# Attention's products with values at the end of a step and one step later, with out-projection chunks moved one step and q's projection over five steps

## The chip, the cores and the metric

The kernel runs on one core of one Trainium2 chip, as one launch. The metric is the device time of that launch in microseconds. The median of three runs before the change is 913.32 us (913.21 to 914.18). One further execution was profiled; its own time was 913.42 us.

## What is computed

Two layers on an input of 256 tokens by 1024 features, all in float32. Each layer is a half-weighted SwiGLU block, a mixer, and a second SwiGLU block, with a layer norm after each of the three. The mixer of layer 0 is a bidirectional chunkwise mLSTM, that of layer 1 a windowed attention. The change lies in the attention alone:

```python
def window_attention(x, w_in, sink, w_out):          # 16 query heads, 4 key/value heads of 64
    p = x @ w_in                                      # q | k | v
    ...
    s = jnp.einsum('bnqkgd,bnskd->bnkgqs', q, kw) * (HEAD_DIM ** -0.5)
    s = s - slopes[:, :, None, None] * dist           # ALiBi
    s = jnp.where(valid, s, MASK_VALUE)               # |t - s| <= 128
    m = jnp.maximum(jnp.max(s, axis=-1, keepdims=True), sink_l)
    pe = jnp.exp(s - m)
    attn = pe / (jnp.sum(pe, axis=-1, keepdims=True) + jnp.exp(sink_l - m))
    o = jnp.einsum('bnkgqs,bnskd->bnqkgd', attn, vw).reshape(B, S, nq)
    return o @ w_out
```

## The kernel before

Float32 accuracy is had from pairs: a float32 operand is split into a rounded high part (a copy on ScalarE) and a low part (a subtraction on VectorE), and a product is three matmuls, high by high, high by low and low by high (`mm3`). Names ending in `_hi` and `_lo` are such pairs. Weights come by DMA into `w_raw` or `s_raw` tiles; `W.high` makes `w_hi` on ScalarE, `W.low` makes `w_lo` on VectorE, and `W.done(.., PU[st], True)` in the attention loop makes up to `PU[st]` high parts, whose low parts follow in `W.lows()`. All engines run their instructions in the order in which the program issues them, so the order of the Python code is the order of each queue. Most vector, scalar and tensor calls go through a recording helper and carry its line, L180; tiles are told apart by their names.

The attention (`attn`) treats the 16 heads as eight pairs j. The first part projects k, v and the first four pairs of q. Then a hand-written software pipeline of eleven steps st runs (L1552 to L1586). A pair goes through four stages, one step apart:

- `scores(j)` in step j: twelve short matmuls of 64 rows into two PSUM banks (`pw<-kT,q`), then on VectorE four fused bias, mask and minimum operations per pair (`sc`, `nm`), then on ScalarE four exponentials with row sums (`sc<-sc,nm`), and `es`.
- `scale(j)` in step j+1: the reciprocal of the sum, and on GpSimd four multiplications of 128 by 256 (`sc<-sc,sm`, L1489). Except for pair 0, the sum and the reciprocal are on GpSimd too (L1485, L1486).
- `turn(j, sb, p)` in step j+2, for sb 0 and 1: four transposes on TensorE (`pw<-ident,sc`), a copy on ScalarE (`pr` high) and a subtraction on VectorE (`pr` low). In steps 2 to 7 the first turn stands ahead of the scores of the step and the second one in the midst of `scores`, after its matmuls (`between`).
- `values(j)` in step j+3, as the first thing of that step: twelve matmuls with v (`pw<-pr,v`), whose result is copied into the place of q's pair j in `qT` (`q_hi<-pw` on ScalarE, `q_lo<-pw` on VectorE).

These stages take their PSUM tiles from `wbank`, four banks in one rotation (`pw`); q's projection and the accumulators of the out-projection take theirs from `ybank` (`py`). A bank is taken again once its last reader is done.

What is left of TensorE's time in a step is filled by `work`, a list of small parts from `fill`. For steps 0 to 3 these are parts of `q_rest`, which projects q's pairs 4 to 7: part i is one `mm3` with 256 columns (three matmuls `py<-xT,w`), 32 parts in all, and every eighth part ends in a copy and a subtraction into `qT`. Parts 0 to 5 run ahead of the loop, and `QC` (L33) says where each step begins: parts 6 to 11 in step 0, 12 to 19 in step 1, 20 to 27 in step 2 and 28 to 31 in step 3. In steps 4 to 10 the parts are those of `out_proj` for chunk c = st - 4: one part is an `mm3` with 512 columns for one half of the tokens and one half of the outputs (`py<-w,q`), four parts for chunks 0 and 1 (`CT`) and two for the others. Of the parts of a step, the first `FB[st]` stand ahead of the transposes (L36), the rest at the end.

After the loop, `tail` adds what is left of the out-projection and does the layer norm. The second feed-forward block of the layer follows.

Of the kernel before, what the change touches and what calls it, by code (L numbers as in the profile page):

```python
# [9 lines left out]
F32 = mybir.dt.float32  # L10
# [19 lines left out]
FIRST = 12  # L30
RING = 10
PU = [2, 0, 1, 2, 1, 2, 1, 1, 0, 1, 2, 4]
QC = [2, 12, 20, 28, 32]  # L33
QX = 6
SW = 1
FB = [1, 0, 1, 0, 2, 0, 0, 0, 1, 1, 2]  # L36
CT = [0, 1]
EX = [1, 2, 2, 2, 2, 2, 2, 2]
RS = [0, 0, 1, 0, 1, 0, 0, 0, 0, 0, 0, 3, 0, 0, 1, 0, 1, 0, 1, 0, 0, 0, 2, 0, 0, 0, 1, 0, 1, 2, 0, 0, 0, 1, 0, 0, 2, 0, 1, 1, 0, 0, 0, 0, 2, 2, 0, 1]
# [405 lines left out]
def trunk_kernel(ctx: ExitStack, tc: tile.TileContext, x, ffn_w_in, ffn_w_out, ln_g, ln_b, ml_w_in, ml_gate_b,  # L445
                 ml_norm_g, ml_w_out, at_w_in, at_sink, at_w_out, out):
    nc = Paced(tc.nc)
# [174 lines left out]
    def pair(p, *idx):  # L622
        return p[0][idx], p[1][idx]

    def wbank(shape=(128, 512)):
        return psum.tile(list(shape), F32, name="pw", tag="pw", bufs=4)
# [4 lines left out]
    A = slice(None)  # L631
# [32 lines left out]
    def load_ln(room, l, n):  # L664
        t = []
        for name, w in (("g", ln_g), ("b", ln_b)):
            a = room("ln_" + name)
            src = w[l, n]
            nc.load(a, bass.AP(tensor=src.tensor, offset=src.offset, ap=[[0, 128], [1, D]]))
            t.append(a)  # L670
        return t
# [663 lines left out]
    def attn(l, n, pending, last):  # L1335
        with ExitStack() as ph:
# [3 lines left out]
            def both(shape, name, bufs=1):  # L1340
                return tuple(tile_(shape, FR, name + e, bufs=bufs) for e in ("_hi", "_lo"))
# [30 lines left out]
            qT = both([128, 8, S], "q")  # L1372
# [28 lines left out]
            def k_turn(t):  # L1401
                p = ybank((128, 4, 128))
                for g in range(4):
                    nc.tensor.transpose(p[:, g], kd[t][:, g].rearrange("p a d -> p (a d)"), ident)
                split_evac(pair(kT, A, A, tok(t)), p)

            def q_turn(t):
                p = ybank((128, 4, 128))
                for j in range(4):
                    nc.tensor.transpose(p[:, j], qd[t][:, j], ident)  # L1410
                split_evac(pair(qT, A, slice(0, 4), tok(t)), p)
# [3 lines left out]
            def q_rest(part):  # L1415
                for i in part:
                    g, f, k = i // 16, i // 8 % 2, i % 8
                    if k == 0:
                        qpart[g] = (W.take(2) if f == 0 else qpart[g][0], ybank((128, S)))
                    pcs, p = qpart[g]  # L1420
                    mm3(p, pair(pcs[k // 4], A, k % 4, tok(f)), pair(xT, A, k), k == 0, k == 7)
                    if k == 7:
                        split_evac(pair(qT, A, 4 + 2 * g + f), p, qs_col[:, 2 * g + f:2 * g + f + 1])
                        if f == 1:
                            del qpart[g]
# [5 lines left out]
            def flush(n):  # L1431

                for d, src in lows[:n]:
                    nc.vector.tensor_sub(d[1], src, d[0].bitcast(F32))
                del lows[:n]
# [43 lines left out]
            def scale(j):  # L1479
                sm, es = stat.pop(j)  # L1480
                if j == 0:
                    nc.vector.tensor_add(sm, sm, es)
                    nc.vector.reciprocal(sm, sm)
                else:
                    nc.gpsimd.tensor_add(sm, sm, es)  # L1485
                    nc.gpsimd.tensor_tensor(sm, sm, minus_one, op=OP.pow)  # L1486
                for t in range(2):
                    for a in range(2):
                        nc.gpsimd.tensor_scalar(sc[j, t][:, a], sc[j, t][:, a], sm[:, t, a:a + 1], 1.0,  # L1489
                                                op0=OP.mult, op1=OP.mult)  # L1490

            def turn(j, sb, p):
                for t in range(2):
                    for a in range(2):
                        nc.tensor.transpose(p[:, a, tok(t)], sc[j, t][:, a, tok(sb)], ident)
                r = W.room(f"pr{sb}", TAGS[2 + sb]).bitcast(FR).rearrange("p (e a s) -> p e a s", e=2, a=2)
                d = (r[:, 0], r[:, 1])
                nc.scalar.copy(d[0], p)
                lows.append((d, p))
                pr[j, sb] = d  # L1500

            lows, sums = [], {}

            def values(j):
                p = wbank((128, S))
                terms = [(sb, a, e, f) for sb in range(2) for e, f in ((0, 0), (1, 0), (0, 1)) for a in range(2)]
                for n_, (sb, a, e, f) in enumerate(terms):
                    v = va[sb][:, j // 2].rearrange("p s d -> p (s d)")
                    at = 128 * e + 64 * (1 - a)
                    nc.tensor.matmul(p, v[:, at:at + 128], pr[j, sb][f][:, a], start=n_ == 0, stop=n_ == len(terms) - 1)  # L1510
                sums[j] = p
                for sb in range(2):
                    del pr[j, sb]
                    W.back(TAGS[2 + sb], 1)

            y = []

# [2 lines left out]
            def out_part(c, t, o):  # L1520
                if not y:
                    y.extend([ybank() for _ in range(2)] for _ in range(2))
                if c not in wo:
                    wo[c], = W.take_rows(1)
                mm3(y[t][o], pair(qT, A, c, tok(t)), pair(wo[c][1], A, 0, slice(o * 512, o * 512 + 512)), c == 0, False)
# [6 lines left out]
            def parts(f_, *args):  # L1532

                if f_ is q_rest:
                    return [lambda i=i: q_rest([i]) for i in args[0]]
                return [lambda t=t, o=o: out_part(args[0], t, o) for t in args[1] for o in range(2)]
# [8 lines left out]
            k_turn(1)  # L1545
            q_rest(range(QC[0]))
            q_turn(1)
            q_rest(range(QC[0], QX))
            fill = {n_: (q_rest, range(max(QX, QC[n_]), QC[n_ + 1])) for n_ in range(4)}
            for c in range(7):  # L1550
                fill[c + 4] = (out_proj, c, (0, 1) if c in CT else (0,))
            for st in range(11):  # L1552
                if st == 2:
                    gb = load_ln(lambda name: tile_([128, D], F32, name), l, n)
                if 0 <= st - 3 < 8:
                    values(st - 3)
                    o = sums.pop(st - 3)
                    d = pair(qT, A, st - 3)
                    nc.scalar.copy(d[0], o)
                    nc.vector.tensor_sub(d[1], o, d[0].bitcast(F32))  # L1560
                if 0 <= st - 1 < 8:
                    rest()
                    scale(st - 1)
                if st == 8:
                    kT.clear()
                    W.back(TAGS[4], 2)
                late = None
                work = parts(*fill[st]) if st in fill else []
                if 0 <= st - 2 < 8:
                    for f_ in work[:FB[st]]:  # L1570
                        f_()
                    work = work[FB[st]:]
                    p0, p1 = wbank((128, 2, S)), wbank((128, 2, S))
                    turn(st - 2, 0, p0)
                    late = lambda: turn(st - 2, 1, p1)
                    if st >= 8 or not SW:
                        late()
                        late = None
                held = [wo[c][0] for c in wo if c not in CT]
                W.done(min([W.used - (2 if qpart else 0)] + held), PU[st], True)  # L1580
                if st < 8:
                    rest = scores(st, late)
                flush(2)
                W.lows()
                for f_ in work:
                    f_()  # L1586
            nc.scalar.preload_act_table(AF.Silu)
            W.done(0, PU[11])
            wo[7], = W.take_rows(1)
# [7 lines left out]
    for j, (kind, l, i, n) in enumerate(stages):  # L1597
        last = j == len(stages) - 1
        bound[0] = j
        nc.filler = W.fill if kind == "ffn" else None  # L1600
        if kind == "ffn":
            pending = ffn(l, i, n, pending, last)
        elif kind == "mlstm":
            pending = mlstm(l, n, pending, last)
        else:
            pending = attn(l, n, pending, last)
# [29 lines left out]
```

## Time and profile before

| what | value |
|---|---|
| median of the runs | 913.32 us |
| time of the profiled execution | 913.42 us |
| its span, first to last instruction | 911.7 us |
| TensorE matmuls, busy | 902.5 us (99%), 4459 of them |
| VectorE, ScalarE, GpSimd, busy | 804.4, 573.1, 152.5 us |
| matmuls of `values` (`pw<-pr,v`) | 96, first 681.1 us, last 717.6 us |
| exponentials of `scores` | 32, first 671.2 us, last 710.1 us |
| scaling on GpSimd (L1489) | 32, first 675.0 us, last 714.2 us |

Times inside the profile count from the start of the span. The eleven steps lie between 669 and 719 us. A matmul's duration is longer than the distance to the next one, since matmuls overlap in the array; how fast TensorE goes is read from the starts. A row of the view in order of time stands for a run of like instructions that follow each other (xN), with the time from the first one's start to the last one's end; brackets give idle time before it and what ended it. The rows "PEld" are TensorE's weight loads.

### The profile page before, as it was taken

How to read it: one execution, taken by the hardware profiler on the slowest of the kernel's cores; microseconds unless marked ns; L12 is line 12 of the kernel's file. 1: busy time of each engine (PE TensorE's matmuls, PEld its weight loads, DVE VectorE, ACT ScalarE, POOL GpSimd, SP SyncE). 2: the span in 40 equal slices, each digit the busy share in tenths (PEclk: the TensorE clock that was granted, in tenths of full speed). 3: DMA queues.
4: the chain of work that ended last, by engine and by line, in shares of the span. 5: the costliest groups of instructions: out<-in, count | busy, mean ns of one | idle time of the engine just before them, and what ended most of it. 6: DMA issues, size and time to landing. Idle time of an engine off the chain costs nothing.

```text
span 911.7 us, 12563 instructions
## 1 busy us (share of the span) xinstructions
PE 902.5 (99%) x4459; PEld 757.4 (83%) x4459; DVE 804.4 (88%) x971; ACT 573.1 (63%) x793; POOL 152.5 (17%) x192
## 2 busy tenths in 40 slices
PE   9999999999999999999999999999999999999996
PEld 7888888889988888888888888888898888888885
DVE  5999999886799898999888899998869889899886
ACT  5776777356664656776646676764569566676660
POOL 0111123113211011212011111110425301111110
PEclk9999999999999999999999999999999999999999
DMA  8999998546637898997868989986534587899851
GB/s 281 367 328 259 288 274 215 162 137 186 208 111 246 296 234 244 290 285 234 241 193 269 259 257 283 272 223 197 159 119 140 163 293 221 204 298 278 252 138 47
DMA packets 100703, 208.53 MB, mean 229 GB/s; under 512 B 6904, under 2 KB 21264, under 8 KB 100640
## 3 DMA queue, kind: packets, MB, share of 16 engines
q1 hardware_dynamic: 82368, 173.04, 54.2%
q0 software_dynamic: 17696, 33.65, 22.3%
q10 hardware_dynamic: 576, 1.05, 0.3%
q8 instruction: 35, 0.57, 0.3%
q14 instruction: 28, 0.23, 0.1%
HBM read 206.65 MB, written 1.05 MB: 228 GB/s over the span
## 4 chain that ended last, share of the span: by engine, by line
PE 98%; DVE 1%; DMA 0%; issue 0%; DVEq 0%
PE pw L180 64%; PE py L180 35%; DMA x<-in_x_dram 0%; DVE x L180 0%; DVE stats L180 0%; DVEq L1632 0%; DVE mv L180 0%; DVE rs L180 0%
## 5 line engine op out<-in xcount | busy, mean ns | idle before, releaser
L180 DVE TENSOR_TENSOR w_lo<-w_raw,w_hi 128x1024 fp32r<-128x1024 f32 (+1 forms) x213 | 255.2, 1219 | 26.6 <-ACT w_hi L180 24.8
L180 ACT CAST w_hi<-w_raw 128x1024 fp32r<-128x1024 f32 (+1 forms) x213 | 218.9, 1049 | 80.3 <-PE py L180 21.7
L180 DVE TENSOR_TENSOR w_lo<-s_raw,w_hi 128x1024 fp32r<-128x1024 f32 x192 | 228.6, 1219 | 18.3 <-ACT w_hi L180 18.2
L180 ACT CAST w_hi<-s_raw 128x1024 fp32r<-128x1024 f32 x192 | 196.6, 1054 | 58.4 <-PE py L180 23.3
L180 PE MATMUL pw<-w_hi,xT_hi 128*128 128x512 f32 x480 | 189.5, 396 | 0.0
L180 PE MATMUL pw<-w_hi,xT_lo 128*128 128x512 f32 x480 | 187.0, 391 | 0.0
L180 PE MATMUL pw<-w_lo,xT_hi 128*128 128x512 f32 x480 | 186.7, 390 | 0.0
L122 POOL DMA_DIRECT2D s_raw<-in_ffn_w_in_dram x64 | 77.4, 1211 | 484.1 <-DVE s_raw L180 226.3
L180 PE MATMUL py<-w_hi,h_hi 128*128 128x512 f32 x349 | 138.2, 396 | 0.0
L180 PE MATMUL py<-w_hi,h_lo 128*128 128x512 f32 x349 | 136.2, 390 | 0.0
L180 PE MATMUL py<-w_lo,h_hi 128*128 128x512 f32 x349 | 136.0, 390 | 0.0
L180 PEld LDWEIGHTS pw<-w_hi,xT_lo 128*128 128x128 f32 x480 | 90.0, 188 | 19.1
L180 PEld LDWEIGHTS pw<-w_lo,xT_hi 128*128 128x128 f32 x480 | 90.3, 188 | 18.6 <-DVE w_lo L180 1.2
L180 PEld LDWEIGHTS pw<-w_hi,xT_hi 128*128 128x128 f32 x480 | 90.1, 188 | 17.4 <-ACT w_hi L180 0.2
L180 PE MATMUL pw<-w_hi,S_hi 128*128 128x512 f32 x256 | 99.7, 390 | 0.0
L180 PE MATMUL pw<-w_lo,S_hi 128*128 128x512 f32 x256 | 99.7, 389 | 0.0
L180 PE MATMUL pw<-w_hi,S_lo 128*128 128x512 f32 x256 | 99.7, 389 | 0.0
L180 PEld LDWEIGHTS py<-w_hi,h_lo 128*128 128x128 f32 x349 | 65.5, 188 | 14.1
L180 DVE TENSOR_TENSOR s_raw<-s_raw,s_raw 128x1024 f32<-128x1024 f32 x64 | 76.8, 1219 | 0.3
L180 PEld LDWEIGHTS py<-w_lo,h_hi 128*128 128x128 f32 x349 | 65.7, 188 | 13.0
L180 PEld LDWEIGHTS py<-w_hi,h_hi 128*128 128x128 f32 x349 | 65.6, 188 | 12.7
L180 PEld LDWEIGHTS pw<-w_hi,S_lo 128*128 128x128 f32 x256 | 48.1, 188 | 10.0
(205 smaller groups left out, 1122.7 us busy)
## 6 DMA issues: line engine op xcount, KB each, us to landing
s_raw<-in_ffn_w_in_dram SPq DMA_DIRECT2D x96, 512.0 KB, 8.0
w_raw<-in_ffn_w_out_dram SPq DMA_DIRECT2D x88, 512.0 KB, 6.1
w_raw<-in_ffn_w_in_dram SPq DMA_DIRECT2D x64, 512.0 KB, 5.7
s_raw<-in_ffn_w_in_dram POOLq DMA_DIRECT2D x64, 512.0 KB, 8.3
w_raw<-in_ml_w_in_dram SPq DMA_DIRECT2D x24, 512.0 KB, 4.6
w_raw<-in_ffn_w_in_dram SPq DMA_DIRECT2D x32, 256.0 KB, 6.0
w_raw<-in_at_w_in_dram SPq DMA_DIRECT2D x12, 512.0 KB, 4.8
w_raw<-in_ml_w_out_dram SPq DMA_DIRECT2D x8, 512.0 KB, 4.1
```

The costliest lines, as they stand in the source:

```text
L122: self.nc.gpsimd.dma_start(ap, source, accum_op=OP.add)
L180: r = f(out, *args, **kw)
```

## The change

`values(j)` copies its result itself. In steps 3 to 7 it is called as the last thing of the step, after the parts of `work`, where it was called as the first thing; its pair is still st - 3. In steps 8 to 10 it stays at the start, behind `VB[st - 8]` parts of `work` (one in step 8, none in 9 and 10). On TensorE's queue `values(0)` so stands between the parts of step 3 and the first transposes of step 4, where it stood ahead of the transposes of step 3; the same holds for pairs 1 to 4.

The chunks of the out-projection go to the steps in `OC`: chunk 0 in step 5, 1 in 6, 2 in 7, 3 and 4 in 8, 5 in 9 and 6 in 10. Parts 6 to 31 of q's projection are spread over five steps: 6 to 11, 12 to 17, 18 to 23, 24 to 27 and 28 to 31. `FB[4]` is 0, where it was 2. Counts of instructions stay the same on every engine.

```diff
-QC = [2, 12, 20, 28, 32]
+QC = [2, 12, 18, 24, 28, 32]
+OC = [5, 6, 7, 8, 8, 9, 10]
+VB = [1, 0, 0]
...
-FB = [1, 0, 1, 0, 2, 0, 0, 0, 1, 1, 2]
+FB = [1, 0, 1, 0, 0, 0, 0, 0, 1, 1, 2]
...
             def values(j):
...
-                sums[j] = p
                 for sb in range(2):
                     del pr[j, sb]
                     W.back(TAGS[2 + sb], 1)
+                d = pair(qT, A, j)
+                nc.scalar.copy(d[0], p)
+                nc.vector.tensor_sub(d[1], p, d[0].bitcast(F32))
...
-            fill = {n_: (q_rest, range(max(QX, QC[n_]), QC[n_ + 1])) for n_ in range(4)}
+            fill = {n_: parts(q_rest, range(max(QX, QC[n_]), QC[n_ + 1])) for n_ in range(5)}
             for c in range(7):
-                fill[c + 4] = (out_proj, c, (0, 1) if c in CT else (0,))
+                fill.setdefault(OC[c], []).extend(parts(out_proj, c, (0, 1) if c in CT else (0,)))
             for st in range(11):
...
-                if 0 <= st - 3 < 8:
+                work = fill.get(st, [])
+                if st >= 8:
+                    for f_ in work[:VB[st - 8]]:
+                        f_()
+                    work = work[VB[st - 8]:]
                     values(st - 3)
-                    o = sums.pop(st - 3)
-                    d = pair(qT, A, st - 3)
-                    nc.scalar.copy(d[0], o)
-                    nc.vector.tensor_sub(d[1], o, d[0].bitcast(F32))
...
-                work = parts(*fill[st]) if st in fill else []
...
                 W.lows()
                 for f_ in work:
                     f_()
+                if 3 <= st < 8:
+                    values(st - 3)
```

On the queue of SP, which issues the loads, one 512 KB load and one pair of 256 KB loads of the next block's `w_raw` come ahead of `s_raw` loads that they followed before: the tiles of `pr` lie in the rooms of `s_raw`, and are given back where `values` is called. The queue of GpSimd is the same. On ScalarE and VectorE only the places of the copies into `qT` change.

2 lines of the change are left out of this document (1 added, 1 removed).

## The prediction

> **What bounds the kernel.** I read the head of the page first, then the chain of work that ended last, then the busy time by stretches.
>
> ```profile
> span 911.7 us, 12563 instructions
> PE 902.5 (99%) x4459; PEld 757.4 (83%) x4459; DVE 804.4 (88%) x971; ACT 573.1 (63%) x793; POOL 152.5 (17%) x192
> ...
> PE 98%; DVE 1%; DMA 0%; issue 0%; DVEq 0%
> ```
>
> ```profile
> 680.00:700.00 20.00, 20.00 (x154) 17.62 (x153) 18.51 (x47) 19.06 (x56) 11.19 (x23) 1.00 0.40 133
> ```
>
> TensorE is busy 99% of the span, 98% of the final chain is TensorE, and it has no idle time to give away. The second fence is 680 to 700 us, in the midst of the attention's steps (window, length, then busy us and instructions of PE, PEld, DVE, ACT, POOL, the granted clock, DMA share, GB/s): TensorE 20.00 of 20 us, but ScalarE 19.06 and VectorE 18.51. So here three engines are nearly full at once. The change takes no matmul away and adds none; it can only remove or add waits of TensorE, and a wait comes out at the end one for one. Busy time cannot show these waits, since a matmul's record is longer than the step to the next; I take them from distances between starts in the order of time.
>
> **What can be won** is small: the waits inside `values`, twelve matmuls that begin while a low part of `pr` is still being made.
>
> ```profile
> 687.40 0.30 PEld L180 LDWEIGHTS pw<-pr,v 128*128 128x128 f32 x2 [0.19 <-DVE pr L180]
> ```
>
> ```profile
> 681.10 1.60 PE L180 MATMUL pw<-pr,v 128*128 128x256 f32 x12
> 682.54 0.60 PE L180 MATMUL pw<-ident,sc 128*128 128x128 f32 x4
> ...
> 685.96 1.94 PE L180 MATMUL pw<-pr,v 128*128 128x256 f32 x12
> 687.74 0.40 PE L180 MATMUL py<-w_hi,q_hi 128*128 128x512 f32 x1
> ...
> 692.45 1.80 PE L180 MATMUL pw<-pr,v 128*128 128x256 f32 x12
> ...
> 703.50 1.80 PE L180 MATMUL pw<-pr,v 128*128 128x256 f32 x12
> ...
> 708.47 1.80 PE L180 MATMUL pw<-pr,v 128*128 128x256 f32 x12
> ```
>
> The first call (pair 0) runs without a wait: 1.60 us, and 682.54 - 681.10 = 1.44 us from its start to the next work. Against 1.60, pair 1 loses 0.34 us, and pairs 2, 4 and 5 0.20 us each. One step later their `pr` is long done, so at most 0.94 us can come back. That is 0.1% of the run.
>
> **What it costs, first place: step 2.** The transposes of step 2 need pair 0 scaled by GpSimd.
>
> ```profile
> 675.02 1.85 POOL L1489 TENSOR_SCALAR sc<-sc,sm 128x256 f32<-128x256 f32 x4 [16.34 <-DVE sm L180]
> ```
>
> ```profile
> 676.55 0.71 PE L180 MATMUL pw<-ident,sc 128*128 128x128 f32 x4
> 677.18 0.39 PE L180 MATMUL pw<-kT_hi,q_hi 64*128 64x256 f32 x2
> ```
>
> ```profile
> 674.08 0.48 DVE L180 SCALAR_TENSOR_TENSOR q_lo<-py,qs_col,q_hi 128x256 fp32r<-128x256 f32 x1
> ```
>
> The four scalings end at 676.87, one every 0.46 us; the four transposes start at 676.55 and take 0.71, against 0.60 at 682.54. So today TensorE arrives just as the last scaling ends: two queues in step, no slack. With `QC` cut from eight parts to six in step 1, TensorE has two parts less ahead of these transposes. A part costs 0.36 us (twelve matmuls, four parts, from 684.45 to 685.96 in the rows further down, less 0.08 for the first). GpSimd does not come earlier: it waits for VectorE's `sm`, which follows the `q_lo` at 674.08 and the work ahead of it, and nothing on any engine is changed up to there. TensorE comes 0.72 us earlier and waits 0.72.
>
> **Second place: step 3.** Its first transposes wait for pair 1 in the same way.
>
> ```profile
> 678.87 0.20 POOL L1485 TENSOR_TENSOR sm<-sm,es 128x4 f32<-128x4 f32 x1 [2.00 <-ACT es L180]
> ...
> 680.29 1.84 POOL L1489 TENSOR_SCALAR sc<-sc,sm 128x256 f32<-128x256 f32 x4
> ```
>
> Today TensorE reaches them at 682.54, after the scalings (680.29 + 1.84 = 682.13). In the new order the two further parts that left step 2 (0.72) and `values(0)` (1.44) are no longer ahead of them, and TensorE is there 2.16 us earlier, at 680.38. GpSimd's start hangs on ScalarE's `es`, behind exponentials of pair 1 that nothing moves. The fourth transpose can start at 682.19, a semaphore's 0.06 us after 682.13; today it starts at about 682.87 (the scores follow at 683.07, 0.2 later). With 0.1 us to refill the array after a wait, the scores of step 3 start at 682.45, 0.62 before today's 683.07. But four parts (1.44) and `values(0)` (1.44) have not been done by then. Loss so far: 2.88 - 0.62 = 2.26 us, 0.72 of it from step 2.
>
> **Third place: the bank of `values(0)` in step 4.** The second transposes of a step take the bank that the last `values` filled, and wait until VectorE's `q_lo<-pw` has read it. This wait exists today, by a hair:
>
> ```profile
> 684.03 0.42 PEld L180 LDWEIGHTS pw<-ident,sc 128*128 128x128 f32 x4 [0.19 <-DVE q_lo L180]
> ```
>
> ```profile
> 683.04 0.35 ACT L180 CAST q_hi<-pw 128x256 fp32r<-128x256 f32 x1
> 683.29 0.48 ACT L180 ACTIVATE es<-nm,sink 128x2 f32<-128x2 f32 x2
> 683.67 0.57 ACT L180 CAST pr<-pw 128x512 fp32r<-128x512 f32 x1
> 684.14 2.00 ACT L180 CAST w_hi<-w_raw 128x1024 fp32r<-128x1024 f32 x2
> 686.03 0.58 ACT L180 CAST pr<-pw 128x512 fp32r<-128x512 f32 x1
> 686.51 0.52 ACT L180 ACTIVATE sc<-sc,nm 128x256 f32<-128x256 f32 x1
> ...
> 688.50 0.47 ACT L180 ACTIVATE q_hi<-py,qs_col 128x256 fp32r<-128x256 f32 x1
> ```
>
> ```profile
> 686.65 0.69 DVE L180 TENSOR_TENSOR pr<-pw,pr 128x512 fp32r<-128x512 f32 x1 [0.15 <-ACT pr L180]
> 687.26 2.35 DVE L180 TENSOR_TENSOR w_lo<-w_raw,w_hi 128x1024 fp32r<-128x1024 f32 x2
> 689.53 0.48 DVE L180 SCALAR_TENSOR_TENSOR q_lo<-py,qs_col,q_hi 128x256 fp32r<-128x256 f32 x1
> 689.92 0.41 DVE L180 TENSOR_TENSOR q_lo<-pw,q_hi 128x256 fp32r<-128x256 f32 x1
> ```
>
> Today the copy of pair 0 stands early: after the exponentials of step 2, ahead of everything of step 3. Its place is now that of the last row, behind all of step 3. On ScalarE, with the `q_hi<-pw` gone from 683.04 (0.25 us), the first `pr` copy starts at 683.42, two `w_hi` end at 685.89, the second `pr` at 686.36. On VectorE then: `pr` low until 687.00, two `w_lo` 2.27 us more (687.26 to 689.53), `q_lo<-pw` 0.41: done at 689.69. (On ScalarE four exponentials, 1.99 us, and `q_hi` end at 688.6, in time.) The transposes can start at 689.75.
>
> ```profile
> 683.07 0.39 PE L180 MATMUL pw<-kT_hi,q_hi 64*128 64x256 f32 x2
> ...
> 684.04 0.66 PE L180 MATMUL pw<-ident,sc 128*128 128x128 f32 x4
> 684.45 0.36 PE L180 MATMUL py<-xT_hi,w_hi 128*128 128x256 f32 x1
> ...
> 689.12 0.60 PE L180 MATMUL pw<-ident,sc 128*128 128x128 f32 x4
> ...
> 690.57 0.66 PE L180 MATMUL pw<-ident,sc 128*128 128x128 f32 x4
> ```
>
> TensorE's arrival, from 682.45: scores 0.91 (683.07 to 684.04 less today's wait of 0.06), transposes 0.41, four parts 1.51, `values(0)` 1.44, first transposes of step 4 0.53, scores 0.91: 688.16. It waits 1.59 us, with the scores of pair 4 already done and everything else queued behind it: its own copy of `pr`, the four parts of step 4, `values(1)`.
>
> Balance there: 689.75 against 690.57 today, 0.82 earlier, with four parts (1.43), `values(1)` (1.44) and two out-projection parts (687.74 to 689.12, 1.38) still to do. 4.25 - 0.82 = 3.43 us behind. Today's waits up to that point, pair 1's 0.34 among them, are already in this.
>
> **After that.** Of today's later waits, pairs 2, 4 and 5 give back 0.60. In steps 5 and 6 the same bank is level.
>
> ```profile
> L180 DVE CUSTOM_DVE_ANT_0 sc<-pw,dist,neg_sink 128x256 f32<-128x256 f32 x32 | 14.0, 479 | 2.7 <-PE pw L180 2.1 <-POOL sm L1485 0.6
> ```
>
> From one `q_lo<-pw` to the next, with one `w_lo` between them, VectorE needs four `sc` of 14.0/32 = 0.44, two `pr` of 0.61, the `w_lo` of 1.13 and two `q_lo` of 0.4: 4.9 us; TensorE, from second transposes to second transposes with the four parts of step 4, needs 0.41 + 1.51 + 1.44 + 0.53 + 0.91 = 4.8. In the next round VectorE has two `w_lo`, 6.0, and TensorE the four out-projection parts of step 5 (2.75) instead of 1.51: 6.0. I take 0.1 for both together, between 0 and 0.5. In step 7 TensorE has the same 6.0 us, and VectorE one `w_lo` less. From `values(6)` on TensorE's order is the old one, so the loss is carried to the end.
>
> The loads that now come later are the `s_raw` ones, a step at most, some 5 us.
>
> ```profile
> L180 ACT CAST w_hi<-s_raw x14: 1049/1052/1061, 748.9 to 787.8; 128x1024 fp32r<-128x1024 f32 x14
> ...
> L118 SPq DMA_DIRECT2D s_raw<-in_ffn_w_in_dram x12: 367/463/840, 711.3 to 779.9; - x12
> ```
>
> Issued from 711.3, first read at 748.9: nothing. Without that cover, 5 us. The copies into `qT` are as many as before.
>
> **Sum:** 3.43 - 0.60 + 0.1 = +2.9 us. From the profiled 913.42 that is 916.3; the median, 913.32, lies 0.1 lower, which changes nothing. Two parts could still be wrong by their bounds: the two early waits (2.26) by 0.4, if a transpose follows its scaling by more or less than 0.06; the third by 0.5, the length of half a `w_lo`. Own range: 915.4 to 917.2.
>
> **Rivals.**
>
> *The bank wait comes back in steps 5 and 6.* For it: VectorE's and TensorE's sums are within 0.1 us there, and VectorE's include no wait of its own. Against: in step 4 it starts late by a whole step, in the later ones only by what is left. If it falls behind by half a `w_lo` (0.6) in both, +1.1: 917.4. Chance 0.11.
>
> *The third wait does not come about.* If the transposes of step 4 got a bank other than that of `values(0)`, 1.59 us fall away: 914.7, within 0.2%. For it: four banks rotate. Against: the row at 684.03, where today's order, too, waits for `q_lo`. Chance 0.09.
>
> *Not slower: GpSimd and ScalarE move forward along with TensorE.* The place is the scaling of pairs 0 and 1. If its start came 0.7 us earlier in step 2, and 1.5 earlier in step 3, nothing would be lost, the bank would be free too, and 0.94 us is won: 912.5. It decides from the point where `sm` starts before 674.5. Against: everything ahead of it keeps its place. Chance 0.04.
>
> *The clock drops.* At the start of the span TensorE runs at half pace:
>
> ```profile
> 1.71 3.25 PE L180 MATMUL py<-ident 128*128 128x128 f32 x14 [1.71 <-DVE ident L180]
> ...
> 5.87 1.04 PE L180 MATMUL py<-ident 128*128 128x128 f32 x8
> ```
>
> Fourteen transposes take 3.25 us there, eight take 1.04 a little later. Should the waits of steps 2 to 4, with transposes between them, bring such a stretch back once, 3.5 us at half pace cost 1.7: 918.0. Against: the longest wait is 1.6 us, and the granted clock is 1.00 in this stretch. Chance 0.05. The Trainium skill, "TensorE: Matmul & The Clock Gate", part 1, speaks against this change in just this way: it puts the fall to half clock after an idle window of about 3.4 us. By that rule waits of 1.6 us with matmuls between them are too short, so it would agree with 916.3 and not with 918.0; its remark that transposes do not count as full activity leaves some doubt.
>
> **Chances.** Forecast 0.68, bank in steps 5 and 6 0.11, clock 0.05, no third wait 0.09, not slower 0.04; 0.03 for what I have not seen, 0.02 of it faster. A change under 0.2% (1.8 us) can't be told from none by a measurement of this kernel. Slower: 0.68 + 0.11 + 0.05 = 0.84; same: 0.09 + 0.04 + 0.01 = 0.14; faster 0.02. The range takes in both neighbours: 914.6 to 917.9.
>
> **What would show it.** In the new profile: the four transposes of step 2 about 0.45 us apart, at GpSimd's pace, beginning near 676; the same in step 3, ending near 682.2; and in step 4 a gap of 1.4 to 1.7 us ahead of the second transposes, ended by VectorE's `q_lo`. No `pw<-pr,v` of pairs 1 to 5 should wait for `pr`. I am wrong if GpSimd's scalings move by more than 0.2 us in steps 2 and 3, or if waits appear outside steps 2 to 6.

## The result and the profile after

The changed kernel takes 916.29 us (median; 915.76 to 918.92), beside it the kernel before 913.86 us (913.21 to 914.79): 1.0036 times as long, 95% interval 1.0023 to 1.0049. It is slower, and the forecast of 916.3 us holds. That the median meets it to 0.01 us is luck: beside it the kernel before took 913.86 us and not the 913.32 that the forecast went by, so the difference is 2.43 us, where 2.9 was forecast. The profiled execution took 917.62 us, though, more than the median and more than the forecast, and its profile shows where. First the head of the page and the shares of the final chain.

```profile
span 915.9 us, 12561 instructions
PE 904.6 (99%) x4459; PEld 759.6 (83%) x4459; DVE 804.5 (88%) x971; ACT 574.2 (63%) x793; POOL 152.9 (17%) x192
...
PE 95%; DVE 3%; issue 1%; POOL 0%; ACT 0%; DVEq 0%; POOLq 0%
```

The work is the same and TensorE again "99% busy"; only the chain tells that something is lost, with TensorE at 95% of it instead of 98%. Now the rows that the forecast named, the transposes of steps 2, 3 and 4, and those of step 5, in the order of time on TensorE (in the changed kernel the recording helper's line is L182, and the scaling's L1491):

```profile
675.42 1.42 PE L182 MATMUL pw<-ident,sc 128*128 128x128 f32 x4
...
680.40 1.23 PE L182 MATMUL pw<-ident,sc 128*128 128x128 f32 x3 [0.29 <-POOL sc L1491]
682.80 0.47 PE L182 MATMUL pw<-ident,sc 128*128 128x128 f32 x1 [1.16 <-POOL sc L1491]
...
690.57 0.66 PE L182 MATMUL pw<-ident,sc 128*128 128x128 f32 x4 [0.34 <-DVE q_lo L182]
...
695.61 0.66 PE L182 MATMUL pw<-ident,sc 128*128 128x128 f32 x4 [0.18 <-DVE q_lo L182]
```

Step 2 is as forecast: four transposes in 1.42 us, at GpSimd's pace, from 675.42. In step 3 only three of four are. The fourth waits 1.16 us more, and the windows from there (length, then busy us and instructions of TensorE, its weight loads, VectorE, ScalarE, GpSimd, and the granted clock, DMA share and GB/s) show a half clock behind it:

```profile
678.00:680.40 2.40, 2.12 (x19) 1.91 (x16) 2.37 (x9) 2.40 (x7) 1.77 (x4) 1.00 0.76 304
680.40:682.60 2.20, 0.98 (x3) 0.41 (x3) 2.08 (x4) 2.20 (x9) 2.20 (x3) 1.00 0.00 0
682.60:686.00 3.40, 3.20 (x19) 2.76 (x20) 1.49 (x6) 3.02 (x7) 2.81 (x7) 0.50 0.43 154
686.00:690.00 4.00, 4.00 (x40) 3.83 (x39) 4.00 (x8) 3.68 (x13) 0.66 (x2) 1.00 0.00 0
```

Why the fourth scaling is late stands in the rows of GpSimd and VectorE of the same time:

```profile
679.87 2.87 POOL L1491 TENSOR_SCALAR sc<-sc,sm 128x256 f32<-128x256 f32 x4
```

```profile
681.25 1.23 DVE L182 TENSOR_TENSOR w_lo<-w_raw,w_hi 128x1024 fp32r<-128x1024 f32 x1
```

The four scalings took 1.84 us before and take 2.87 here: the last of them met a `w_lo` of VectorE and stood for its length. The kernel before has the same meeting, but there it is the `w_lo` that is held up, 1.53 us instead of 1.23:

```profile
681.67 1.53 DVE L180 TENSOR_TENSOR w_lo<-w_raw,w_hi 128x1024 fp32r<-128x1024 f32 x1
```

So this one execution holds the forecast's three waits, plus a meeting of two engines that went the other way and a half clock. The experiments take these apart.

### The profile page after: what moved, and what is told of

It reads as the page before. It is cut to its first block, busy times and chain, and to the rows that moved or that the text cites. A ratio compares the mean times of both kernels' runs of the same rounds, so it can differ in the third digit from the quotient of the medians.

```text
span 915.9 us, 12561 instructions
## 1 busy us (share of the span) xinstructions
PE 904.6 (99%) x4459; PEld 759.6 (83%) x4459; DVE 804.5 (88%) x971; ACT 574.2 (63%) x793; POOL 152.9 (17%) x192
## 4 chain that ended last, share of the span: by engine, by line
PE 95%; DVE 3%; issue 1%; POOL 0%; ACT 0%; DVEq 0%; POOLq 0%
PE pw L182 62%; PE py L182 34%; DVE w_lo L182 1%; DVE sc L182 1%; ACT sc L182 0%; POOL sc L1491 0%; DVE x L182 0%; DVE pr L182 0%; DVE stats L182 0%; DVE q_lo L182 0%; DVE e L182 0%; DVE s_raw L182 0%; POOL sm L1488 0%; ACT q_hi L182 0%; DVEq L1637 0%
## 5 line engine op out<-in xcount | busy, mean ns | idle before, releaser
L182 DVE TENSOR_TENSOR w_lo<-w_raw,w_hi 128x1024 fp32r<-128x1024 f32 (+1 forms) x213 | 255.1, 1218 | 24.3 <-ACT w_hi L182 22.3
L182 ACT CAST w_hi<-w_raw 128x1024 fp32r<-128x1024 f32 (+1 forms) x213 | 219.1, 1049 | 78.8 <-PE py L182 22.2
L182 DVE TENSOR_TENSOR w_lo<-s_raw,w_hi 128x1024 fp32r<-128x1024 f32 x192 | 228.8, 1221 | 18.5 <-ACT w_hi L182 18.5
L182 ACT CAST w_hi<-s_raw 128x1024 fp32r<-128x1024 f32 x192 | 196.6, 1054 | 58.1 <-PE py L182 22.7
L182 PE MATMUL pw<-w_hi,xT_hi 128*128 128x512 f32 x480 | 189.5, 396 | 0.0
L182 PE MATMUL pw<-w_hi,xT_lo 128*128 128x512 f32 x480 | 186.9, 391 | 0.0
L182 PE MATMUL pw<-w_lo,xT_hi 128*128 128x512 f32 x480 | 186.5, 390 | 0.2 <-DVE w_lo L182 0.2
L182 PE MATMUL py<-w_hi,h_hi 128*128 128x512 f32 x349 | 138.2, 396 | 0.0
L182 PE MATMUL py<-w_hi,h_lo 128*128 128x512 f32 x349 | 136.2, 390 | 0.0
L182 PE MATMUL py<-w_lo,h_hi 128*128 128x512 f32 x349 | 135.9, 390 | 0.0
L182 PEld LDWEIGHTS pw<-w_hi,xT_lo 128*128 128x128 f32 x480 | 90.1, 188 | 19.1
L182 PEld LDWEIGHTS pw<-w_lo,xT_hi 128*128 128x128 f32 x480 | 90.3, 188 | 18.8 <-DVE w_lo L182 1.1
L182 PEld LDWEIGHTS pw<-w_hi,xT_hi 128*128 128x128 f32 x480 | 90.0, 188 | 17.3
L182 PE MATMUL pw<-w_hi,S_lo 128*128 128x512 f32 x256 | 99.7, 389 | 0.0
L182 PE MATMUL pw<-w_hi,S_hi 128*128 128x512 f32 x256 | 99.7, 389 | 0.0
L182 PE MATMUL pw<-w_lo,S_hi 128*128 128x512 f32 x256 | 99.7, 389 | 0.0
L182 PEld LDWEIGHTS py<-w_hi,h_lo 128*128 128x128 f32 x349 | 65.5, 188 | 14.0
L182 DVE TENSOR_TENSOR s_raw<-s_raw,s_raw 128x1024 f32<-128x1024 f32 x64 | 76.8, 1220 | 0.3
L182 PEld LDWEIGHTS py<-w_lo,h_hi 128*128 128x128 f32 x349 | 65.7, 188 | 13.0
L182 PEld LDWEIGHTS py<-w_hi,h_hi 128*128 128x128 f32 x349 | 65.6, 188 | 12.8
L182 PEld LDWEIGHTS pw<-w_lo,S_hi 128*128 128x128 f32 x256 | 48.1, 188 | 10.0
```

Source lines behind the costliest of these rows:

```text
L182: r = f(out, *args, **kw)
```

## The experiments

Whole times can't show a few tenths here. The eleven steps begin at another moment in each execution, from 668.07 to 671.10 us in the fourteen profiles of this case, though the work ahead of them is the same. So parts are compared by one stretch: from the first scores of step 0 to the first product of the last block's second half. Before, it is 902.36 - 669.05 = 233.31 us:

```profile
669.05 0.39 PE L180 MATMUL pw<-kT_hi,q_hi 64*128 64x256 f32 x2
...
902.36 0.28 PE L180 MATMUL pw<-w_hi,h_hi 128*128 128x256 f32 x1
```

In the profiled execution of the changed kernel it is 237.95, 4.64 more. This stretch reaches past the attention, whose end is seen in the transposes `py<-ident,x` behind its last product:

```profile
727.28 1.04 PE L180 MATMUL py<-ident,x 128*128 128x128 f32 x8
```

Before, they start 727.28 - 669.05 = 58.23 us after the first scores, in the changed kernel 731.05 - 668.64 = 62.41. So 4.18 of the 4.64 us arise in the attention and 0.46 behind it. Where nothing else is said, what a profile has more than 233.31 us arises in the attention, to within 0.01.

In the expectations, T is the theory that each of the three waits can be had back by itself, R that the vector engines release TensorE at fixed times and that only the work put behind these releases counts, M that the meeting of scaling and `w_lo` explains the longer times.

### How firm the stretch is: the kernel before again

No edit.

> The kernel before, profiled once more, to see how firm the stretch is that the parts are measured by (first scores of step 0 to the last FFN product, 233.31 us in the first profile). If differences of a few tenths in this stretch mean anything, it comes out at 233.1 to 233.5, whatever the time of the whole run; where it differs by more than 0.5, the readings of single profiles so far carry no order among them.

Measured: 233.27 us, 0.04 from the first profile; the whole time 913.13 us beside 913.39 (0.9996, 0.9987 to 1.0005). Its steps began 0.98 us earlier than in the first profile, and the stretch did not care. Differences of a few tenths in it can be read.

### The changed kernel again

No edit.

> The changed kernel once more. Theory of the prediction (T): three waits of TensorE, in steps 2, 3 and 4, together some 2.9 us: 915.9 to 916.3. Theory of the meeting (M), for what lies above that: in step 3 GpSimd's fourth scaling and VectorE's low part of a weight (w_lo) start within some 25 ns of one another, and whichever starts first holds the other up. Where w_lo is first the scaling takes 1.5 us instead of 0.48, TensorE's last transpose of step 3 comes 1.0 us later, and the clock is at half for 3.4 us behind it: 917.6 to 918.9. Where the scaling is first: 915.8 to 916.3 and the clock at 1.00 all through step 3. M expects one of the two, with scaling length, clock and time going together; a profile with a long scaling and a full clock, or with a short scaling and half a clock, speaks against M.

Measured: 917.01 us beside 913.44 (1.0034, 1.0024 to 1.0045). Its profile has the short scalings and the full clock:

```profile
670.66 0.39 PE L182 MATMUL pw<-kT_hi,q_hi 64*128 64x256 f32 x2
...
677.44 1.43 PE L182 MATMUL pw<-ident,sc 128*128 128x128 f32 x4
...
682.43 1.70 PE L182 MATMUL pw<-ident,sc 128*128 128x128 f32 x4 [0.27 <-POOL sc L1491]
...
691.32 0.66 PE L182 MATMUL pw<-ident,sc 128*128 128x128 f32 x4 [1.50 <-DVE q_lo L182]
...
907.14 0.28 PE L182 MATMUL pw<-w_hi,h_hi 128*128 128x256 f32 x1
```

```profile
681.89 1.85 POOL L1491 TENSOR_SCALAR sc<-sc,sm 128x256 f32<-128x256 f32 x4
```

```profile
683.27 1.54 DVE L182 TENSOR_TENSOR w_lo<-w_raw,w_hi 128x1024 fp32r<-128x1024 f32 x1
...
688.59 2.35 DVE L182 TENSOR_TENSOR w_lo<-w_raw,w_hi 128x1024 fp32r<-128x1024 f32 x2
690.85 0.42 DVE L182 TENSOR_TENSOR q_lo<-pw,q_hi 128x256 fp32r<-128x256 f32 x1
```

This is the forecast's picture without accidents in the steps: 236.48 us, 3.17 more than before. At the end of the attention it is 731.82 - 670.66 = 61.16, 2.93 more. The other 0.24 comes 100 us later, in the feed-forward block, where a weight load of TensorE waits for a `w_lo`:

```profile
731.82 1.04 PE L182 MATMUL py<-ident,x 128*128 128x128 f32 x8
```

```profile
831.60 0.19 PEld L182 LDWEIGHTS pw<-w_lo,xT_hi 128*128 128x128 f32 x1 [0.38 <-DVE w_lo L182]
```

Three of the fourteen profiles have this wait: both of the changed kernel, and that of out-projection and q further down. Why these three have it is not known.

In step 3 the scaling won the meeting (four in 1.85), and `w_lo` took 1.54 instead of 1.23, as in the kernel before. So scaling, clock and stretch go together in these two profiles, as M says. But this execution took 918.18 us, as long as the long ones, since its steps began 1.61 us later than in the first profile of the kernel before. M holds for the stretch; as the account of why whole times lie at 916 or at 918 it falls.

### Without the meeting: a weight split out of step 2

```diff
-PU = [2, 0, 1, 2, 1, 2, 1, 1, 0, 1, 2, 4]
+PU = [2, 0, 0, 2, 1, 2, 1, 1, 1, 1, 2, 4]
```

> The split of one weight is taken out of step 2 and put into step 8, so that VectorE has no w_lo while GpSimd scales pair 1. M: the fourth scaling takes 0.48 us in every run, no half clock in steps 3 and 4, and every time lies at 915.8 to 916.5; none at 917.6 or above. Against M (the clock falls because of the waits alone, the long scaling is beside the point): the half clock stays in some runs, and times of 917.6 to 918.9 stay too. T expects 915.9 to 916.5 either way, since none of the three waits hangs on this split.

Measured: 916.26 us (915.80 to 917.44) beside 913.44, 1.0032 (1.0019 to 1.0044). Four scalings in 1.86 us, clock 1.00 through the steps, stretch 236.25, 2.94 more than before. Single times of 916.92 and 917.44 lie above what M allowed, so M again does not order the whole times. What does follow: with the split gone from step 2 the loss in the attention is the same (2.94 here, 2.93 above), so neither meeting nor half clock is part of the 2.9 that was forecast. The split that was moved meets the scalings of the last pair instead, and these take 2.81 us from 714.61; no wait of TensorE is recorded there.

### The third wait taken away: another bank

```diff
-                p = wbank((128, S))
+                p = (ybank if j < 2 else wbank)((128, S))
```

> values(0) and values(1) take their bank from the parts' banks, so that the second transposes of steps 4 and 5 no longer wait for VectorE's q_lo to read it. T (three separate terms, each of which can be taken away alone): the third wait's 1.6 us fall away, 914.3 to 914.8. Rival R (the pace of VectorE, ScalarE and GpSimd in steps 2 to 6 sets the end; TensorE has lost the work it would do meanwhile, and the waits only change place): 915.9 to 916.3 as the changed kernel has, with the gap ahead of the second transposes of step 4 gone and new gaps of about the same sum within steps 4 to 6, ahead of the first transposes or of the values.

Measured: 916.47 us beside 913.44, 1.0033 (1.0020 to 1.0046); stretch 236.07, 2.76 more. The second transposes of step 4 run without a wait, at 690.19, and yet only 0.17 of the 2.93 us in the attention comes back:

```profile
690.19 0.66 PE L182 MATMUL pw<-ident,sc 128*128 128x128 f32 x4
693.56 1.31 PE L182 MATMUL pw<-ident,sc 128*128 128x128 f32 x4
695.71 0.65 PE L182 MATMUL pw<-ident,sc 128*128 128x128 f32 x4
700.38 0.60 PE L182 MATMUL pw<-ident,sc 128*128 128x128 f32 x4
702.78 0.66 PE L182 MATMUL pw<-ident,sc 128*128 128x128 f32 x4 [0.89 <-DVE q_lo L182]
```

```profile
692.63 1.85 POOL L1491 TENSOR_SCALAR sc<-sc,sm 128x256 f32<-128x256 f32 x4
```

The first transposes of step 5 now come at the pace of GpSimd's scalings, the last row (1.31 us against 0.60), and the second transposes of step 6 wait 0.89 us for the `q_lo` of a later pair, the third wait two steps later. T falls. R has it right that the wait comes back in steps 5 and 6 in about its old size (0.71 and 0.89 us); the time is 0.2 above R's 916.3.

### The first wait taken away: q's projection back

```diff
-QC = [2, 12, 18, 24, 28, 32]
+QC = [2, 12, 20, 28, 32, 32]
```

> q's projection goes back to its old places (eight parts in steps 1 and 2, four in step 3, none in step 4); values and out-projection stay late. T: the 0.72 us of step 2 fall away and nothing else: 915.2 to 915.6. R: the wait of step 2 is gone, but those of steps 4 and 5 grow by as much, since the four parts of step 4 are not there to fill them: 915.9 to 916.3.

Measured: 916.92 us beside 913.44, 1.0034 (1.0022 to 1.0047); stretch 236.86, 3.55 more. The transposes of step 2 take 0.72 us as before, and the wait of step 4 grows:

```profile
677.03 0.72 PE L182 MATMUL pw<-ident,sc 128*128 128x128 f32 x4
...
690.60 0.66 PE L182 MATMUL pw<-ident,sc 128*128 128x128 f32 x4 [1.89 <-DVE q_lo L182]
691.50 2.90 PE L182 MATMUL pw<-pr,v 128*128 128x256 f32 x12 [0.24 <-DVE nm L182]
```

T's 0.72 does not come back. R's gap grew less than R said (1.89 against 1.50), and the time is 0.6 above R's 916.3. In this profile the clock fell behind the wait, too: `values` took 2.90 us instead of 1.60. How much of the time that explains was not tried.

### One part of the change at a time

Out-projection alone, as the change from the kernel above with q's projection back:

```diff
+                if 3 <= st < 8:
+                    values(st - 3)
                 if 0 <= st - 1 < 8:
                     rest()
...
-                if 3 <= st < 8:
-                    values(st - 3)
```

> The out-projection part alone: its chunks come one step later as in the changed kernel, and step 4 has no parts of it ahead of the transposes; values come first in their step and q's projection is where it was before. Measured as the change of the stretch from the first scores of step 0 to the last FFN product, against the kernel before (233.3 us there). T (the prediction's three terms, each by itself): none of the three waits is due, since values(0) and q's parts stand where they stood: +0.0 to +0.3. R (steps 2 to 6 go at the pace of VectorE, ScalarE and GpSimd; what TensorE loses is the work taken from those steps, wherever it waits): +1.4 to +2.0, nearly the 2.75 us of chunk 0 that leaves step 4 less what TensorE is ahead, with a wait of over 1 us ahead of the second transposes of step 4.

The same edit with q's projection as changed, so that values alone is undone:

> The changed kernel with values first in steps 3 to 7 as before; out-projection and q's projection as changed. Same measure as above. T: the first term (0.72 of step 2) is left alone, and the copy of values(0) stands early, so that no third wait is due: +0.7 to +1.0. R: +1.8 to +2.2, no more than 0.4 above the out-projection part alone, since the wait of step 2 takes the place of waits in steps 3 and 4.

Values alone at the end of the step, from the changed kernel:

```diff
-QC = [2, 12, 18, 24, 28, 32]
-OC = [5, 6, 7, 8, 8, 9, 10]
-VB = [1, 0, 0]
+QC = [2, 12, 20, 28, 32, 32]
+OC = [4, 5, 6, 7, 8, 9, 10]
+VB = [0, 0, 0]
```

> Values alone at the end of the step: q's projection as before, out-projection chunks in their old steps, but none of their parts ahead of the transposes of step 4, since these now read what values writes. Same measure. T: the second and third terms, 1.5 and 1.6: +2.2 to +3.1, and the three parts of the change added up then exceed the whole. R: +1.9 to +2.4, one wait of about 2 us in step 4; with the out-projection part alone at 1.8 the two add to about 4, and the whole change is at 3: the waits are shared, not summed.

q's projection alone, from the kernel before:

```diff
-QC = [2, 12, 20, 28, 32]
+QC = [2, 12, 18, 24, 28, 32]
...
-            fill = {n_: (q_rest, range(max(QX, QC[n_]), QC[n_ + 1])) for n_ in range(4)}
+            fill = {n_: parts(q_rest, range(max(QX, QC[n_]), QC[n_ + 1])) for n_ in range(5)}
             for c in range(7):
-                fill[c + 4] = (out_proj, c, (0, 1) if c in CT else (0,))
+                fill.setdefault(c + 4, []).extend(parts(out_proj, c, (0, 1) if c in CT else (0,)))
```

> q's projection over five steps alone; values first in their step and the out-projection chunks where they were before. Same measure. T: the 0.72 us of step 2 and nothing else: +0.7 to +0.9. R: as much again as for the other parts, since TensorE reaches steps 3 to 5 as early as in the whole change: +2.0 to +3.3, with waits in steps 3 and 4 of 0.3 to 0.6 and one of 1 us or more in step 4 or 5, where chunk 0's parts stand behind q's last ones. With out-projection alone at 1.70 and values alone at 1.92 the three would add to 5.6 to 6.9, where the whole change has 2.9 to 3.2.

| kernel | time, us | ratio to before (95%) | stretch, us | more than 233.31 | of it in the attention |
|---|---|---|---|---|---|
| out-projection alone | 915.46 | 1.0018 (1.0009 to 1.0028) | 235.01 | 1.70 | all |
| values alone | 915.99 | 1.0026 (1.0015 to 1.0037) | 235.23 | 1.92 | all |
| q's projection alone | 916.12 | 1.0030 (1.0019 to 1.0040) | 236.43 | 3.12 | all |
| out-projection and q | 915.72 | 1.0025 (1.0015 to 1.0034) | 235.48 | 2.17 | 1.76 |
| all three (second profile) | 917.01 | 1.0034 (1.0024 to 1.0045) | 236.48 | 3.17 | 2.93 |

Each part alone is slower than the kernel before, and the three add up to 6.74 us where the whole has 3.17. They are not three separate pieces, though: in each of these kernels the two out-projection parts that stood ahead of the transposes of step 4 (1.38 us) come behind them, so the sum counts these three times. T had 0.0 to 0.3 for the out-projection, in which none of the three waits is due, 2.2 to 3.1 for values and 0.7 to 0.9 for q. R's bounds for the stretch hold in all four. Two of its details do not: out-projection and q lies 0.47 above out-projection alone instead of at most 0.4 (0.06 in the attention), and q's kernel has no recorded wait ahead of the transposes of step 4. Where the time goes, in the out-projection's, values' and q's own profile:

```profile
690.55 0.65 PE L182 MATMUL pw<-ident,sc 128*128 128x128 f32 x4 [1.14 <-DVE q_lo L182]
...
693.36 0.51 PE L182 MATMUL pw<-pr,v 128*128 128x256 f32 x2 [0.43 <-DVE pr L182]
```

```profile
691.85 0.66 PE L182 MATMUL pw<-ident,sc 128*128 128x128 f32 x4 [1.90 <-DVE q_lo L182]
```

```profile
695.28 0.50 PE L180 MATMUL py<-w_hi,q_hi 128*128 128x512 f32 x1 [1.52 <-DVE q_lo L180]
```

The first two wait at the place of the third wait, though in the out-projection's kernel the copy of `values` stands early, as it did before the change; there pair 2 then waits for its `pr` as well. The last waits for a different bank: chunk 0 takes over that of q's last part, which VectorE reads at 694.74 to 695.22.

### VectorE and ScalarE relieved ahead of the third wait

A weight split is a `w_hi` on ScalarE and a `w_lo` on VectorE. Both splits of step 3 later (a), or one of them (b), in the changed kernel; one of them in the kernel before (c):

```diff
-PU = [2, 0, 1, 2, 1, 2, 1, 1, 0, 1, 2, 4]
+PU = [2, 0, 1, 0, 1, 2, 1, 1, 1, 2, 2, 4]
```

```diff
-PU = [2, 0, 1, 2, 1, 2, 1, 1, 0, 1, 2, 4]
+PU = [2, 0, 1, 1, 1, 2, 1, 1, 1, 1, 2, 4]
```

> The changed kernel with the two weight splits of step 3 moved to steps 8 and 9: VectorE has two w_lo of 1.15 us less, ScalarE two w_hi less, ahead of the q_lo that step 4's second transposes wait for. Same measure; the changed kernel has +2.9 to +3.2 where no half clock falls into it. T: the third term goes, 1.6 us less: +1.3 to +1.6. R, if VectorE is the pace: the wait of step 4 goes from 2 us to under 0.4, a part of it comes back as waits in step 5 (0.4) and, where the moved splits now stand, ahead of the FFN (0.6): +2.4 to +2.8.

> The changed kernel with one of step 3's two weight splits moved to step 8: one w_lo (1.15 us) less on VectorE, one w_hi less on ScalarE, before the second transposes of step 4. Same measure; the changed kernel has +3.17 without a half clock, and +2.39 with both splits moved, of which 0.54 is a wait that the second one makes ahead of the FFN. If VectorE's queue is what TensorE waits for in step 4, nearly the whole w_lo comes back: +1.7 to +2.1, the wait of step 4 under 0.3 and the one ahead of the FFN gone. If something else is as late (GpSimd's scalings, ScalarE's exponentials), the wait only changes its place: +2.7 to +3.2.

> The same move of one weight split in the kernel before, as a candidate that might be quicker than both: TensorE waits there only within values, 0.94 us in all, 0.34 of it for pair 1, whose low part stands behind that w_lo. If VectorE is the pace in step 3 of this kernel too: the wait of pair 1 goes, -0.2 to -0.4 in the stretch, 913.0 to 913.3. If the moved split costs elsewhere what it gives here: 0.0.

Measured, (a): 916.60 us beside 913.49, 1.0030 (1.0019 to 1.0041), stretch 235.70, 2.39 more, near R's 2.4 and far from T's 1.3 to 1.6. (b): 915.03 beside 913.39, 1.0017 (1.0008 to 1.0026), stretch 235.03, 1.72 more. In (b), VectorE and TensorE around step 4:

```profile
686.83 1.50 DVE L182 TENSOR_TENSOR w_lo<-w_raw,w_hi 128x1024 fp32r<-128x1024 f32 x1
688.25 0.41 DVE L182 TENSOR_TENSOR q_lo<-pw,q_hi 128x256 fp32r<-128x256 f32 x1
```

```profile
688.72 0.66 PE L182 MATMUL pw<-ident,sc 128*128 128x128 f32 x4
...
693.99 0.66 PE L182 MATMUL pw<-ident,sc 128*128 128x128 f32 x4 [0.40 <-DVE q_lo L182]
```

One split less ahead of `q_lo`, and 1.21 us of the 2.93 in the attention are gone. Not all of that is the missing `w_lo`. In the second profile of the changed kernel VectorE stands 0.49 us for a `pr` that ScalarE copies behind two `w_hi`; in (b), with one `w_hi`, it does not:

```profile
687.98 0.69 DVE L182 TENSOR_TENSOR pr<-pw,pr 128x512 fp32r<-128x512 f32 x1 [0.49 <-ACT pr L182]
```

```profile
686.23 0.68 DVE L182 TENSOR_TENSOR pr<-pw,pr 128x512 fp32r<-128x512 f32 x1
```

Counted from the first scores this `pr` starts 0.59 us earlier in (b) (16.73 against 17.32). From the first `w_lo` to `q_lo` it is then 1.42 us instead of 2.26, 0.84 less, and the transposes come 1.44 earlier in all. So this wait is VectorE's queue together with ScalarE's ahead of it, shown by taking work out of both; neither was relieved alone. (a) takes out one more, which does nothing more at step 4 (the second transposes start 19.20 us after the first scores, 19.22 in (b)) and costs ahead of the FFN, where it now stands:

```profile
722.74 0.50 PE L182 MATMUL py<-w_hi,q_lo 128*128 128x512 f32 x1 [0.38 <-DVE q_lo L182]
```

(c): 914.06 beside 913.39, 1.0004 (0.9995 to 1.0013), stretch 233.81, 0.50 more; outside both values that were expected. Pair 1's `values` do lose less, 1.72 us against 1.94, but step 9 pays:

```profile
714.66 0.38 PE L180 MATMUL pw<-ident,sc 128*128 128x128 f32 x2
715.29 1.22 PE L180 MATMUL pw<-ident,sc 128*128 128x128 f32 x6 [0.25 <-POOL sc L1489]
```

```profile
712.88 2.80 POOL L1489 TENSOR_SCALAR sc<-sc,sm 128x256 f32<-128x256 f32 x4
```

```profile
713.59 1.30 DVE L180 TENSOR_TENSOR w_lo<-w_raw,w_hi 128x1024 fp32r<-128x1024 f32 x1
```

The moved `w_lo` meets the last scaling of pair 7, four scalings take 2.80 us, and the transposes of step 9 wait for it. No version that was run beats the kernel before.

## Why the prediction was right

By its own steps, in the second profile of the changed kernel, which has no accident in the steps:

1. *What can be won, 0.94.* Pairs 1 to 5 run their `values` in 1.60 us without waits for `pr`. Right. Pair 6 gains 0.12 as well (1.59 against 1.71), which the forecast did not count.
2. *Step 2, 0.72.* The second profile's first transposes start 6.78 us after the first scores, 7.50 before: 0.72 earlier, and the second transposes follow at 9.05 and 9.04. All of it is lost. GpSimd has not moved: its scalings begin 5.97 us after the first scores in both (676.63 - 670.66 and 675.02 - 669.05), and in step 3 11.23 and 11.24. Right.
3. *Step 3.* Second transposes at 14.30 (684.96 - 670.66) against 14.99 (684.04 - 669.05): 0.69 earlier. The forecast had 0.62 plus 0.06 for today's small wait. Right.
4. *Step 4, third wait 1.59.* The gap is 1.50 us by the row, and 1.56 by distances between starts: 2.47 from the first scores (688.85) to the transposes, less the 0.91 that the forecast took for this. It ends 20.66 us after the first scores (691.32 - 670.66), against 21.52 before (690.57 - 669.05): 0.86 earlier, where the forecast had 0.82. Released by `q_lo` behind two `w_lo`, as named. Right.
5. *Steps 5 and 6, 0.1.* Step 5 waits for its `q_lo` too, as the row of the first profile shows (0.18). By distances between starts, the way the forecast counted, it is 0.24 in the second profile: 1.15 us from the first scores to the transposes, less 0.91:

```profile
695.22 0.39 PE L182 MATMUL pw<-kT_hi,q_hi 64*128 64x256 f32 x2
...
696.37 0.66 PE L182 MATMUL pw<-ident,sc 128*128 128x128 f32 x4 [0.18 <-DVE q_lo L182]
```

   Mis-sized by 0.14, within the 0 to 0.5 that was given; nothing in step 6.
6. *Sum.* 4.25 us of work moved behind the release, less 0.86: 3.39; less 0.60 given back, and 0.12 more by pair 6: 2.67; plus 0.24 in step 5: 2.91. Measured at the end of the attention 2.93, forecast 2.9. That it is so close is partly luck, since the two small errors, step 5 and pair 6, cancel.

The forecast had named a wait outside steps 2 to 6 as a sign of being wrong, and the feed-forward block has one, 0.24 us of the stretch. None of the six steps hangs on it, but the forecast did not see it.

Wrong was a rival's price. "The third wait does not come about" was put at 914.7, by taking the wait off the sum. With the wait removed the stretch is 236.07, which with the 913.42 - 233.31 that lie outside it makes 916.2. And the clock, held against by "the longest wait is 1.6 us", did fall in two of the eleven profiles of changed kernels, the first of the changed kernel and that with q's projection back. In the first, meeting and clock together cost 4.18 - 2.93 = 1.25 us in the attention, where the rival had 1.7 for the clock alone. The rows from the start of the span that it went by don't show the clock: the view of windows has a granted clock of 1.00 there.

Why the sum was right and the price wrong is one and the same thing. The forecast's balance doesn't add waits: it takes the moment at which a release comes, and the work that is then still to do. The same form, worked out afterwards, goes some way for the other kernels too, with 1.43 for four parts of q's projection, half of it for two, 1.44 for `values(1)` and 1.38 for two out-projection parts:

| kernel | second transposes of step 4, us after first scores | earlier than 21.52 | work put behind them | balance | measured in the attention |
|---|---|---|---|---|---|
| all three | 20.66 | 0.86 | 4.25 | 3.39 | 2.93 |
| out-projection alone | 21.33 | 0.19 | 1.38 | 1.19 | 1.70 |
| values alone | 21.07 | 0.45 | 2.82 | 2.37 | 1.92 |
| out-projection and q | 20.95 | 0.57 | 2.81 | 2.24 | 1.76 |
| one split later (b) | 19.22 | 2.30 | 4.25 | 1.95 | 1.72 |
| other bank | 19.09 | 2.43 | 4.25 | 1.82 | 2.76 |
| q's projection alone | 20.95 | 0.57 | 2.10 | 1.53 | 3.12 |

Where balance and measurement differ, later waits make the difference: they are won back (values alone, 0.60 of `pr` waits), come anew (other bank; q's projection alone, with its wait of 1.52), or stay within `values` (out-projection alone, where pair 2 still waits for `pr`). That was added up to the end only for all three (2.91 against 2.93); for the others it is read from the rows. In the first four rows the transposes wait for `q_lo`, and the release lies between 20.66 and 21.33: the queues of VectorE and ScalarE set it. What is taken from in front of it is lost, once, whichever part takes it; so the parts don't add up, and a wait that is removed only lets TensorE run on to the next release. That these two queues hold the release is shown by (b), for both together. That GpSimd's scalings hold the next one is seen in the other bank's profile, and was not tried by relieving GpSimd.

## What to carry to other kernels

Where several engines are nearly full, price a move by a balance at the next release: how much work of the bounding engine now lies behind it, less how much earlier the release comes. Don't price it by the waits, nor take one off the sum to see what its removal gives, since the next release has its own time. Measure such effects over the stretch that the change touches, not over the whole run, where the start alone wandered by 3 us here. Let the stretch end where the changed part ends: a wait 100 us behind it added 0.24 to 0.46 us in three profiles.

## What was not expected of the hardware

**A scaling and a `w_lo` that start within some 0.02 us of one another: one of them stands for most of the other's length, and either may win.** In the second profile of the changed kernel `w_lo` took 1.54 us instead of 1.23 and the scalings were untouched (1.85); in the first the four scalings took 2.87 instead of 1.84 and `w_lo` was untouched. All profiles but that without the split in step 2 have this meeting, the kernel before too; `w_lo` was held up in twelve of the thirteen. The Trainium skill, "SBUF — State Buffer", section "SBUF: two separate sides", has an exclusive lock between VectorE, with two inputs in SBUF, and a GpSimd operation that reads it, held for the whole instruction. The traces agree roughly: 1.03 us lost against a `w_lo` of 1.23, 0.31 against a scaling of 0.46. Its rule that the one that starts first has the lock can't be read from the records: with one scaling every 0.45 us, the fourth starts at 681.23 and 683.25 in the two profiles, 0.02 ahead of `w_lo` (681.25 and 683.27) in both, and it won in one.

**The clock fell to half after waits much shorter than its own stretch.** In the first profile of the changed kernel, 2.20 us with TensorE busy for 0.98 were enough (the windows above). In the kernel with q's projection back it was this:

```profile
688.00:690.60 2.60, 0.71 (x12) 0.51 (x11) 2.60 (x5) 2.60 (x10) 0.62 (x2) 1.00 0.26 90
690.60:691.30 0.70, 0.66 (x4) 0.42 (x4) 0.70 (x5) 0.63 (x1) 0.60 (x2) 0.98 0.99 386
691.30:694.70 3.40, 3.20 (x15) 3.23 (x16) 3.20 (x9) 2.94 (x10) 1.84 (x4) 0.50 0.50 165
```

Both times the half clock lasted 3.4 us. Values alone had a wait as long as this one (1.90 us against 1.89) and kept its clock, so the length of the wait alone doesn't decide it. The Trainium skill, "TensorE: Matmul & The Clock Gate", part 1, speaks of a free-running activity window of about 3.4 us; a fall that depends on how the gap lies to such a window would look like this, but no run here shows the window itself. Its rule of about 3.4 us of idle time is too wide for these rows: a wait of 1.89 us was followed by half clock.
